# Second branch's keys and queries as four normed pairs with seven quarter products, on one Trainium2 core

## The chip, the core and the metric

The kernel runs on one core of a Trainium2 chip. A core has a matrix engine (TensorE, PE in the profile, with its weight loads PEld), three engines for elementwise work (VectorE or DVE, ScalarE or ACT, GpSimd or POOL) and SyncE (SP), which here only issues transfers. Every engine works through its own queue in order. TensorE writes to PSUM, eight banks of 2 KB in each of 128 partitions; the other memory on the core is SBUF. The metric is the device time of one execution in microseconds, lower is better.

## The reference: one layer of a hybrid encoder

A prompt of 1024 new frames and 64 frames of a running stream (1088 tokens, T in the code) go through one layer of width 1024. The part around the change is the input projection and the per-head norm of the second ("chunk-band", cb) branch:

```python
h = rms_norm(x, norm_w) @ w_in                 # 1024 -> 6144 columns
sb_q, sb_k, sb_v, sb_z, cb_q, cb_k, cb_v, cb_z, g_sb, g_cb = split(h)
cb_q = rms_norm(cb_q.reshape(lead + (8, 64)), q_norm_w)   # per head of 64
cb_k = rms_norm(cb_k.reshape(lead + (8, 64)), k_norm_w)
...
s = q @ k.T * 0.125 + rel_bias[clip(q_pos - k_pos)]       # cb branch
y = x + (sigmoid(g_sb) * b_sb + sigmoid(g_cb) * b_cb) @ w_out
```

The keys and values of both branches are outputs too; of the cb branch only the last 512 prompt frames and the 64 stream frames. Products are held to float32 accuracy: an operand is split into a high part and a low part (the rest of the subtraction), and three of the four products of parts are summed on TensorE.

## The kernel before, in words

Each engine's order is the order in which the code issues its instructions; there is no planner. The work around the change has two stages ahead of the attention.

**The natural stage** (the loop around L466, "natural" since tokens are on the partitions). List `NB` names eight blocks of 256 columns of `w_in`: one of sb values, two of cb keys, two of cb queries, one of sb values, two of cb values. A block runs over nine token tiles (the 64 stream frames first). A tile of 128 frames takes 24 matmuls of 256 columns into one PSUM bank (L466), the stream tile 16. Values are copied out by ACT and stored. Keys and queries go through `evac_nat` (copy, square, per-head sum, `rsqrt` on POOL), `norm_nat` (two multiplications on DVE) and, some tiles later, `post_nat` (two transposes on PE at L351, and the split into high and low part), and are stored transposed to DRAM. During the first block the frames are normed and transposed; the cached keys are transposed in blocks 1 to 4 (`cache_pair`). From the sixth block on `make_t` makes, on DVE and ACT, four sums of quarters of the transposed frames (t0 to t3), with their split.

**The pair stage** (L632 on, the loop at L651). `pairs` lists 14 pairs of 128-column groups: keys and queries of the sb branch, the gates and others. A pair is a product of a 2x2 block matrix of weights (256 columns by 1024) with a 2x2 block matrix of frames (1024 by two halves of 544 tokens). It is done in seven quarter products, s = 0 to 6, in place of eight, at the price of sums: `presum` makes the weight sums on DVE, six products ahead; `prep` splits them on ACT and POOL, five ahead. A quarter product is 2 column chunks (c = 0, 1; 256 and 288 tokens) of 12 matmuls (L672). There are six PSUM banks, three for each chunk, one buffer each: bank 1 takes products 0 and 3, bank 2 takes 1, 4 and 5, bank 3 takes 2 and 6. DVE reads a bank between the products that share it, so the product that comes next into that bank waits on PE until DVE has read. The tightest such place is bank 2 between s = 4 and s = 5: `u3` of chunk 0 (L680) is to be read while PE does chunk 1 of s = 4. Finished results go to `emit`: split, store by SP one product later, and for keys a transposition back through PSUM tile `acc` (pool `psF`, two buffers). From the fifth pair on `dv_step` also makes differences of the sb values.

The relative-position bias is laid out in DRAM as eight arrays of 128 equal rows (`d_rb`), which the attention reads with a skew: `load_rb` spreads the table over 128 partitions, `make_rb` writes the negated and clamped row with DVE and stores it, head by head.

The lines below are the functions that the change touches.

Of the kernel before, what the change touches and what calls it, by code (L numbers as in the profile page):

```python
# [8 lines left out]
F32 = mybir.dt.float32  # L9
# [9 lines left out]
NP = 1024  # L19
# [13 lines left out]
def hybrid_step_kernel(ctx: ExitStack, tc: tile.TileContext, x_prompt, x_sample, c_sbk, c_sbv, c_cbk, c_cbv,  # L33
# [49 lines left out]
    d_o = {b: [dram.tile([128, T], F32, name=f"d_o{b}{p}") for p in range(NPAIR)] for b in ("sb", "cb")}  # L83
    d_rb = [dram.tile([128, 768], F32, name=f"d_rb{h}") for h in range(8)]
# [62 lines left out]
    for p in (0, 2):  # L147
        pairs += [("k", 512 + 128 * p, p), ("q", 128 * p, p)]
# [51 lines left out]
    with ExitStack() as ph:  # L200
        sx = ExitStack()
        natx = sx.enter_context(tc.tile_pool(name="natx", bufs=2))
        pn = ph.enter_context(tc.tile_pool(name="pn", bufs=2, side="right"))
        p1x = ExitStack()
# [5 lines left out]
        NB = [1024, 2560, 2816, 2048, 2304, 1280, 3072, 3328]  # L210
        nb = len(NB)
        xts, xns, hl, cks = {}, {}, {}, {}
# [21 lines left out]
        wqk = pn.tile([128, 2, 64], F32, name="wqk", bufs=1)  # L234
# [3 lines left out]
        def load_rb():  # L238
            rbs[0] = p1.tile([128, 8, 257], F32, name="ck", bufs=1)
            SP.dma_start(rbs[0], rel_bias[0:1].to_broadcast([128, 8, 257]))  # L240

        def make_rb(h):
            rb = rbs[0]
            rx = p1.tile([128, 768], F32, name="rx", bufs=3)
            V.tensor_scalar(rx[:, 0:512], rb[:, h, 256:257].to_broadcast([128, 512]), -1.0, None, op0=OP.mult)
            V.tensor_scalar(rx[:, 512:768], rb[:, h, 255::-1], -1.0, None, op0=OP.mult)
            SP.dma_start(d_rb[h], rx)
# [50 lines left out]
        def evac_nat(i, t, ps):  # L298
            r = rows(t)
            if t == 8:  # L300
                ps = fold(pn, ps)
            c0 = NB[i]
            grp = c0 // 512
            n0 = c0 % 512
            if grp in (2, 6):
                v = pn.tile([128, 256], F32, name="vst", bufs=3)
                A.activation(v[:r], ps[:r, :], AF.Copy)
                dst = d_sbv if grp == 2 else d_cbv
                SP.dma_start(dst[t * 128:t * 128 + r, n0:n0 + 256], v[:r])
                if grp == 2:  # L310
                    SP.dma_start(tok(o_sbv_p, o_sbv_s, t)[:, n0:n0 + 256], v[:r])
                elif t == 8:
                    SP.dma_start(o_cbv_s[:, n0:n0 + 256], v[:r])
                elif t >= 4:
                    SP.dma_start(o_cbv_p[(t - 4) * 128:(t - 3) * 128, n0:n0 + 256], v[:r])
                return
            sq = p1.tile([128, 256], F32, name="sqn")
            ms = p1.tile([128, 4], F32, name="msn")
            rs = p1.tile([128, 4], F32, name="rsn", bufs=3)
            qn = p1.tile([128, 4, 64], F32, name="qn", bufs=5)  # L320
            A.activation(qn[:r].rearrange("p h d -> p (h d)"), ps[:r, :], AF.Copy)
            A.activation(sq[:r], ps[:r, :], AF.Square)
            V.tensor_reduce(ms[:r], sq[:r].rearrange("p (h d) -> p h d", d=64), axis=AX.X, op=OP.add)
            rsqrt(rs[:r], ms[:r], 1.0 / 64, 4)
            return qn, rs

        def norm_nat(i, t, qn, rs):
            r = rows(t)
            n0 = NB[i] % 512
            isk = 1 if NB[i] // 512 == 5 else 0  # L330
            V.tensor_tensor(out=qn[:r], in0=qn[:r], in1=rs[:r, :, None].to_broadcast([r, 4, 64]), op=OP.mult)
            V.tensor_tensor(out=qn[:r], in0=qn[:r], in1=wqk[:r, None, isk, :].to_broadcast([r, 4, 64]),
                            op=OP.mult)
            if isk:
                if t == 8:
                    SP.dma_start(o_cbk_s[:, n0:n0 + 256], qn[:r].rearrange("p h d -> p (h d)"))
                elif t >= 4:
                    SP.dma_start(o_cbk_p[(t - 4) * 128:(t - 3) * 128, n0:n0 + 256],
                                 qn[:r].rearrange("p h d -> p (h d)"))

        def post_nat(i, t, qn):
            r = rows(t)
            c0 = NB[i]
            isk = 1 if c0 // 512 == 5 else 0
            p0 = (c0 % 512) // 128
            if t in (8, 4):
                hl[0] = p1.tile([128, 2, 2, 576], F32R, name="hl", bufs=3)
            h = hl[0]
            pt = psK.tile([128, 2, 128], F32, name="pk")
            for j in range(2):  # L350
                TE.transpose(pt[:, j, :r], qn[:r].rearrange("p h d -> p (h d)")[:, j * 128:(j + 1) * 128],  # L351
                             ident[:r, :r])
            c = 512 if t == 8 else (t % 4) * 128
            o = slice(c, c + r)
            A.activation(h[:, :, 0, o], pt[:, :, :r], AF.Copy)
            V.tensor_tensor(out=h[:, :, 1, o], in0=pt[:, :, :r], in1=h[:, :, 0, o].bitcast(F32), op=OP.subtract)
            dst = (d_kT if isk else d_qT)["cb"]
            if t in (3, 7):
                for j in range(2):
                    rdma(dst[p0 + j][:, :, (t - 3) * 128:(t + 1) * 128], h[:, j, :, 0:512])  # L360
                    if t == 3:
                        rdma(dst[p0 + j][:, :, NP:T], h[:, j, :, 512:576])
# [1211 lines left out]
```

## Time and profile before

| | us |
|---|---|
| median of 3 runs (985.72 to 988.01) | 986.68 |
| the profiled execution | 985.0 |
| its span in the profile | 983.2 |
| granted TensorE clock | 1.0 |

The profile is of one execution. "Busy" is the time in which an engine had an instruction at work; a row of a group of instructions gives the line, the engine, output and inputs by the program's names, partitions by elements, the count, the busy sum and the mean of one in ns, and behind the second bar the idle time ahead of them and what ended it. The chain of work that ended last is followed back from the last instruction. The natural stage runs from the start to 226 us, the pair stage from 226 to 524 us, and the attention and the last products take the rest.

### The profile page before, as it was taken

The numbers are of one execution on the slowest core, as the hardware profiler recorded it, in microseconds if no ns is written. First come the engines' busy times: TensorE is split into PE (matmuls) and PEld (weight loads), VectorE is DVE, ScalarE is ACT, GpSimd is POOL, SyncE is SP. The second block draws the span as 40 slices with busy tenths as digits, with TensorE's granted clock in tenths as the row PEclk, the third lists the DMA queues.
The fourth block names the chain that finished last, engine by engine and source line by source line (L and its number), as shares of the span: only waits on it lengthen the run. The fifth ranks groups of instructions, "written<-read, shape, count | busy, mean of one in ns | idle before, by whom it ended". The sixth has DMA issues, their size and how long they took to land.

```text
span 983.2 us, 20553 instructions
## 1 busy us (share of the span) xinstructions
PE 957.4 (97%) x7620; PEld 913.0 (93%) x7620; DVE 594.5 (60%) x1168; ACT 479.3 (49%) x1056; POOL 394.1 (40%) x389
## 2 busy tenths in 40 slices
PE   5999999999999999999999899998999999999998
PEld 5999999999999999999999788887888887999998
DVE  5456664796454655533322479776677765689745
ACT  6544443344443433433332567666886875466320
POOL 3276664115444576556523100111421101486551
PEclk9999999999999999999999999999999999999999
DMA  6727567533656565565424999667798862762642
GB/s 230 229 89 239 193 234 255 161 98 120 183 178 199 157 184 169 151 196 173 128 73 127 263 225 250 175 185 184 212 269 238 227 177 84 236 201 74 219 131 76
DMA packets 176585, 176.82 MB, mean 180 GB/s; under 512 B 33825, under 2 KB 160669, under 8 KB 176358
## 3 DMA queue, kind: packets, MB, share of 16 engines
q1 hardware_dynamic: 164950, 160.50, 55.7%
q10 hardware_dynamic: 8720, 8.33, 2.6%
q0 software_dynamic: 2816, 6.69, 2.0%
q8 instruction: 60, 0.98, 0.5%
q14 instruction: 39, 0.32, 0.1%
HBM read 113.46 MB, written 62.00 MB: 178 GB/s over the span
## 4 chain that ended last, share of the span: by engine, by line
PE 89%; ACT 3%; DMA 2%; SPq 2%; DVE 2%; issue 1%; POOL 1%; DVEq 0%; ACTq 0%; POOLq 0%
PE b L672 30%; PE acc L466 19%; PE b L1488 8%; PE o L1172 7%; PE pt L1133 6%; PE z L1080 6%; PE b L974 5%; PE acc L932 4%; PE acc L832 2%; SPq L51 1%; ACT wT L1142 1%; DMA wrawx<-in_w_in_dram 1%; PE pk L351 1%; DMA ks<-d_ksbT 1%; PE pt L279 1%
## 5 line engine op out<-in xcount | busy, mean ns | idle before, releaser
L1133 PE MATMUL pt<-ident,be 128*128 128x128 f32 (+1 forms) x568 | 87.5, 278 | 6.2 <-DVE sm L1085 1.8
L1080 PE MATMUL z<-ks,sq 128*128 128x320 f32 (+5 forms) x384 | 84.9, 330 | 1.8 <-DMA sq<-d_qsbT 1.5
L1102 DVE TENSOR_TENSOR_SCAN be<-be,imp 128x128 f32<-128x128 f32 (+7 forms) x64 | 83.4, 1341 | 5.2 <-ACT be L1083 5.1
L1133 PEld LDWEIGHTS pt<-ident,be 128*128 128x128 f32 (+1 forms) x568 | 65.2, 140 | 18.8 <-issue 5.7
L1142 ACT ACTIVATE wT<-pt 128x512 f32<-128x512 f32 (+3 forms) x125 | 57.1, 485 | 49.3 <-PE pt L1133 48.0
L466 PE MATMUL acc<-whi,xa 128*128 128x256 f32 x256 | 74.2, 292 | 0.0
L466 PE MATMUL acc<-wlox,xm 128*128 128x256 f32 x256 | 70.7, 278 | 0.0
L466 PE MATMUL acc<-whi,xm 128*128 128x256 f32 x256 | 70.7, 278 | 0.0
L466 PE MATMUL acc<-wlo,xa 128*128 128x256 f32 x256 | 70.7, 278 | 0.0
L466 PE MATMUL acc<-whix,xb 128*128 128x256 f32 x256 | 70.6, 278 | 0.0
L466 PE MATMUL acc<-whix,xm 128*128 128x256 f32 x256 | 70.6, 278 | 0.0
L680 DVE TENSOR_TENSOR u<-b,s 128x256 f32<-128x256 f32 (+1 forms) x56 | 24.2, 440 | 73.4 <-PE b L672 71.9
L1080 PEld LDWEIGHTS z<-ks,sq 128*128 128x128 f32 x384 | 64.8, 189 | 3.5 <-DMA sq<-d_qsbT 1.2
L1172 PE MATMUL o<-wT,vp 128*64 128x256 f32 (+1 forms) x608 | 66.6, 357 | 0.1
L1172 PEld LDWEIGHTS o<-wT,vp 128*64 128x64 f32 x608 | 43.9, 136 | 22.9 <-issue 5.5
L123 POOL TENSOR_TENSOR wlo<-wraw,whi 128x1024 fp32r<-128x1024 f32 x15 | 36.6, 2437 | 51.6 <-ACT whi L116 46.4
L745 POOL DMA_DIRECT2D d_osb<-zt x20 | 10.8, 542 | 114.3 <-DVE zt L1181 102.9
L1105 ACT ACTIVATE be<-be,sm 128x640 f32<-128x640 f32 (+5 forms) x68 | 47.2, 694 | 9.7 <-DVE sm L1104 9.5
L436 POOL TENSOR_TENSOR whix<-ws,whix 128x512 fp32r<-128x512 f32 x28 | 37.1, 1324 | 32.5 <-ACT whix L435 32.5
L1083 ACT ACTIVATE be<-z 128x384 f32<-128x384 f32 (+6 forms) x104 | 47.2, 492 | 3.9 <-PE z L1080 3.4
L1093 ACT ACTIVATE be<-be,sm 128x640 f32<-128x640 f32 (+5 forms) x68 | 47.2, 695 | 3.5 <-DVE sm L1085 3.0
L466 PEld LDWEIGHTS acc<-whi,xa 128*128 128x128 f32 x256 | 47.9, 188 | 0.1
(306 smaller groups left out, 3196.3 us busy)
## 6 DMA issues: line engine op xcount, KB each, us to landing
wraw<-in_w_in_dram SPq DMA_DIRECT2D x31, 512.0 KB, 4.4
wrawx<-in_w_in_dram SPq DMA_DIRECT2D x17, 512.0 KB, 4.3
sq<-d_qsbT SPq DMA_DIRECT2D x32, 192.0 KB, 6.2
sq<-d_qcbT SPq DMA_DIRECT2D x32, 192.0 KB, 5.4
xt<-in_x_prompt_dram SPq DMA_DIRECT2D x8, 512.0 KB, 5.8
d_kcbT<-hl SPq DMA_DIRECT2D x8, 512.0 KB, 4.4
d_qcbT<-hl SPq DMA_DIRECT2D x8, 512.0 KB, 3.1
d_ksbT<-hl SPq DMA_DIRECT2D x16, 256.0 KB, 2.7
```

The costliest lines, as they stand in the source:

```text
L466: TE.matmul(ps, x, w, start=m == 0, stop=m == len(steps) - 1)
L672: TE.matmul(ps[:, :m], w[:, hl_, k], right[s](x)[:, k, a:b], start=s < 3 and k == 0 and e == 0, stop=k == 3 and e == 2, skip_group_check=s ...
L974: TE.matmul(pp[uu][:, :n], w[:, p, uu * 128:uu * 128 + 128], g[:, a:e], start=p == 0 and m == 0, stop=p == NPAIR - 1 and m == 2)
L1080: TE.matmul(z[:, :m], s[:, e, q0:q0 + 128], ks[:, h, o + x:o + y], start=e == parts[0][0], stop=e == parts[-1][0])
L1083: A.activation(be[:r, x:y], z[:r, :m], AF.Sigmoid, scale=-0.125)
L1093: A.activation(be[:, :n], be[:, :n], AF.Exp, bias=kp[:, j:j + 1], scale=-1.0, accum_out=kp[:, 2:3])
L1102: V.tensor_tensor_scan(be[:r, n - 1::-1], be[:r, n - 1::-1], im[:, ::-1], 0.0, op0=OP.mult, op1=OP.max)
L1105: A.activation(be[:r, :n], be[:r, :n], AF.Copy, scale=kp[:r, 3:4])
L1133: TE.transpose(pt[:kr, x, :r], be[:r, kb * 128:kb * 128 + kr], ident[:r, :r])
L1142: A.activation(w[:, sl:sl + m, q0:q0 + r], pt[:, :m, :r], AF.Copy)
L1172: TE.matmul(o[hd * 64:hd * 64 + 64, c0:c1], vv[:kr, kb, hd * 64:hd * 64 + 64], wT[b, p, j, hd, s // 4][:kr, s % 4, c0:c1] if j < 4 else wT ...
L1488: TE.matmul(ps[:, t], left[s](xs_, k)[:, ts_], wt_[:, k], start=s < 3 and t == k == e == 0, stop=k == 3 and e == 2, skip_group_check=s > 2 ...
```

## The change

The four natural blocks of cb keys and queries go away. In their place stand four more pairs, `ck` and `cq`, in the pair stage, ahead of and between the sb ones: ck, q, ck, q, cq, k, cq, k. What was done with tokens on the partitions is now done with tokens along the row, on pieces of 128 by 256 or 288 (`normed`):

- `squares`: ACT squares the piece and copies it to a high part, POOL makes the low part;
- `spread`: PE multiplies a block matrix of ones by both parts, so that each row gets the sum over its head of 64, and ACT takes the square root (`Sqrt`, from PSUM);
- `scale`: DVE takes the reciprocal of the 128 by 256 or 288 piece, and multiplies piece, weight and reciprocal in one instruction;
- `parts`: ACT and DVE split, SP stores, and keys that are an output are transposed back (`k_out`).

The four run as a pipe: `norm_step`, called eight times in a pair, issues `parts` of the piece that entered four steps ago, `scale` of the one of three steps ago, `spread` of the one of two steps ago, and `squares` of a new one. So eight pieces of a pair are finished in the first part of the pair behind it. `make_t` moves forward to the second of the now four natural blocks; the cached keys go to the second and fourth. `dv_step` starts with the tenth of 18 pairs. The bias table is loaded on 8 partitions, made there once, stored as `d_r8`, and spread to the eight `d_rb` by transfers within DRAM, one in each of the first eight pairs. Buffers change with it (`hl` 7 for 4, `s1` and `u2` 4, `ko` 3, others shared).

```diff
     for p in (0, 2):
-        pairs += [("k", 512 + 128 * p, p), ("q", 128 * p, p)]
+        pairs += [("ck", 2560 + 128 * p, p), ("q", 128 * p, p)]
+    for p in (0, 2):
+        pairs += [("cq", 2048 + 128 * p, p), ("k", 512 + 128 * p, p)]
...
-        NB = [1024, 2560, 2816, 2048, 2304, 1280, 3072, 3328]
+        NB = [1024, 1280, 3072, 3328]
...
+        def make_rb():
             rb = rbs[0]
-            rx = p1.tile([128, 768], F32, name="rx", bufs=3)
...
+            rx = p2.tile([8, 768], F32, name="rx", bufs=1)
+            V.tensor_scalar(rx[:, 0:512], rb[:, 256:257].to_broadcast([8, 512]), -1.0, None, op0=OP.mult)
+            V.tensor_scalar(rx[:, 512:768], rb[:, 255::-1], -1.0, None, op0=OP.mult)
+            SP.dma_start(d_r8, rx)
+
+        def spread_rb(h):
+            SP.dma_start(d_rb[h], d_r8[h:h + 1].to_broadcast([128, 768]))
...
+            def squares():
+                sq = hold[:, 288 * nsq[0]:288 * nsq[0] + n]
+                nsq[0] = (nsq[0] + 1) % 3
+                h = up.tile([128, 2, 288], F32R, name="hl", bufs=HB)
+                A.activation(sq, x, AF.Square)
+                A.activation(h[:, 0, :n], sq, AF.Copy)
+                G.tensor_tensor(out=h[:, 1, :n], in0=sq, in1=h[:, 0, :n].bitcast(F32), op=OP.subtract)
+                return h
+
+            def spread(h):
+                pt = psF.tile([128, 512], F32, name="acc")[:, :n]
+                for e in range(2):
+                    TE.matmul(pt, ones, h[:, e, :n], start=e == 0, stop=e == 1)
+                rt = up.tile([128, 288], F32, name="rt", bufs=2)
+                A.activation(rt[:, :n], pt, AF.Sqrt, bias=eps64)
+                return rt[:, :n]
+
+            def scale(rt):
+                V.reciprocal(rt, rt)
+                V.scalar_tensor_tensor(x, x, wn[:, 1:2] if isk else wn[:, 0:1], rt, op0=OP.mult, op1=OP.mult)
+
+            def parts():
+                h = up.tile([128, 2, 288], F32R, name="hl", bufs=HB)
+                A.activation(h[:, 0, :n], x, AF.Copy)
+                V.tensor_tensor(out=h[:, 1, :n], in0=x, in1=h[:, 0, :n].bitcast(F32), op=OP.subtract)
+                soon(0, lambda: stores(rdma, half, c, h[:, :, :n], dst[:]))
+                if isk and (half or c):
+                    soon(1, lambda: k_out(src, p, half, c, c * 256 if half else None, o_cbk_p, o_cbk_s))
...
+        def norm_step(late):
+
+            pipe[1:] = pipe[:4]
+            pipe[0] = [norms.pop(1 if late and len(norms) > 1 else 0), None] if norms else None
+            for at, k in ((4, 3), (3, 2), (2, 1), (0, 0)):
+                f = pipe[at]
+                if f:
+                    f[1] = f[0][k](*(f[1:] if k in (1, 2) else ()))
...
-                if i > 3:
+                if i > 8:
                     dv_step(n % 2)
+                if i < 8 and s == 0:
+                    spread_rb(i)
                 w = blk.pop(n)
                 for c, (a, b) in enumerate(XC):
                     m = b - a
+                    if c and s != 4:
+                        norm_step(s == 5 or s == 6)
...
+                if s in (2, 6):
+                    norm_step(False)
```

How this moves instructions shows in two places, both in the second pair (a `q` pair). First DVE, from the end of the first pair to the sum `u` that PE needs before it may start s = 5. Before, the whole stretch is nine instructions (the last of the first pair, the weight sums `ws`, two sums of s = 1, the split of the two results of s = 3, and the sum):

```order
L581 TENSOR_TENSOR hl<-u_3343,hl 128x288
L403 TENSOR_TENSOR ws<-wraw,ws 128x512
L680 TENSOR_TENSOR u_3641<-b_3628,s_3606 128x256
L680 TENSOR_TENSOR u_3656<-b_3643,s_3621 128x288
L403 TENSOR_TENSOR ws<-wraw,wrawx 128x512
L403 TENSOR_TENSOR ws<-ws,wraw 128x512
L581 TENSOR_TENSOR hl<-b_3593,hl 128x256
L581 TENSOR_TENSOR hl<-b_3608,hl 128x288
L680 TENSOR_TENSOR u_3758<-b_3628,s_3606 128x256
```

In the changed kernel the same stretch has 25 on DVE; its last twelve are these (`hl` of L554 are the split of the q pair, the rest are steps of the normed pieces of the ck pair):

```order
L616 TENSOR_TENSOR hl<-u_1887,hl 128x288
L610 RECIPROCAL rt<-rt 128x288
L611 SCALAR_TENSOR_TENSOR kf<-kf,wn,rt 128x288
L616 TENSOR_TENSOR hl<-kf,hl 128x288
L610 RECIPROCAL rt<-rt 128x256
L611 SCALAR_TENSOR_TENSOR s_1738<-s_1738,wn,rt 128x256
L554 TENSOR_TENSOR hl<-b_1982,hl 128x256
L616 TENSOR_TENSOR hl<-s_1738,hl 128x256
L610 RECIPROCAL rt<-rt 128x288
L611 SCALAR_TENSOR_TENSOR s_1753<-s_1753,wn,rt 128x288
L554 TENSOR_TENSOR hl<-b_2011,hl 128x288
L711 TENSOR_TENSOR u_2225<-b_2032,s_1995 128x256
```

Six reciprocals of full pieces, six scalings and five splits have come in ahead of the sum. Second PE, in the same pair at the step from s = 2 to s = 3. Before, the matmuls of one product follow those of the other:

```order
L672 MATMUL b_3694<-t0h,whix 128x288 x2
L672 MATMUL b_3694<-t0l,whix 128x288
L672 MATMUL b_3694<-t0h,whix 128x288 x2
L672 MATMUL b_3694<-t0l,whix 128x288
L672 MATMUL b_3694<-t0h,whix 128x288
L672 MATMUL b_3593<-xm,wlox 128x256
```

Now a spread of squares (`ones`) and a transposition back stand between them:

```order
L703 MATMUL b_2111<-t0h,whix 128x288 x2
L703 MATMUL b_2111<-t0l,whix 128x288
L703 MATMUL b_2111<-t0h,whix 128x288
L604 MATMUL acc<-hl,ones 128x288 x2
L572 MATMUL acc<-ident,u_1873 128x128 x2
L703 MATMUL b_1982<-xm,wlox 128x256
```

Both inserted groups need a buffer of `acc` and a result of other engines, and PE's queue holds them in order.

More of the change, by code (lines that the diff above doesn't have):

```diff
@@ L325, in evac_nat @@
[L325 to L362, printed above, removed]
+            v = pn.tile([128, 256], F32, name="vst", bufs=3)
@@ L590, in emit, with k_out @@
                 V.tensor_copy(kf[:, :n], src[:, :n])
[L592 to L595 removed]
+            soon(2 if (w, half) == (0, 0) else 3,
+                 lambda: k_out(kf, p, half, c, half * 512 + c * 256, o_sbk_p, o_sbk_s))
+        def k_out(kf, p, half, c, a, o_p, o_s):
+            pt = psF.tile([128, 512], F32, name="acc")
+            cols = slice(p * 128, (p + 1) * 128)
+            if a is not None:
```

172 lines of the change are left out of this document (89 added, 83 removed).

## The prediction

> **What bounds the kernel now.** I read the page's busy line first, then the chain that ended last by line:
>
> ```profile
> PE 957.4 (97%) x7620; PEld 913.0 (93%) x7620; DVE 594.5 (60%) x1168; ACT 479.3 (49%) x1056; POOL 394.1 (40%) x389
> PE b L672 30%; PE acc L466 19%; PE b L1488 8%; PE o L1172 7%; PE pt L1133 6%; PE z L1080 6%; PE b L974 5%; PE acc L932 4%; PE acc L832 2%; SPq L51 1%; ACT wT L1142 1%; DMA wrawx<-in_w_in_dram 1%; PE pk L351 1%; DMA ks<-d_ksbT 1%; PE pt L279 1%
> ```
>
> PE carries the time, half of it in the two stages that change (L466 natural, L672 pairs). The view by windows says how much the others have left there: one natural block with keys or queries, the end of `make_t`, and a stretch with a q and a k pair.
>
> ```profile
> 127.00:154.00 27.00, 27.00 (x234) 26.80 (x233) 19.15 (x45) 11.26 (x31) 17.76 (x20) 1.00 0.66 230
> 203.00:226.00 23.00, 23.00 (x205) 23.00 (x204) 22.47 (x33) 9.72 (x21) 1.29 (x1) 1.00 0.32 99
> 250.00:275.00 25.00, 25.00 (x205) 24.99 (x204) 11.49 (x24) 9.49 (x24) 10.72 (x7) 1.00 0.70 210
> 275.00:300.00 25.00, 25.00 (x202) 24.54 (x201) 13.41 (x28) 11.21 (x30) 11.55 (x8) 1.00 0.52 156
> ```
>
> Columns: length, then busy PE, PEld, DVE, ACT, POOL, the granted clock, the DMA share. PE is full in all four; its clock is 1.00. In the pairs DVE has about 12 of 25 us left: what the change lays there must fit into that, and where it comes in a bunch, into less.
>
> **What PE gains.** The chain in order of time gives the pitch of both stages (start, duration, what):
>
> ```profile
> 21.36 0.87 PE pt L279 x8
> ...
> 72.85 1.89 PE acc L466 x16
> ...
> 84.44 2.82 PE acc L466 x24
> ...
> 154.37 1.90 PE acc L466 x16
> ...
> 300.44 223.60 PE b L672 x1800
> ```
>
> The x16 pieces are stream tiles, with which a block begins. Three of the four blocks that go lie between 72.85 and 154.37: 81.5 us, 27.2 a block, where 8 x 2.83 + 1.9 = 24.5 is matmuls and the rest transpositions. Twenty of these are of cached keys and only move: at 0.87/8 = 0.109 us, 2.2 us. So 79.3 us for three, 105.8 for four.
>
> A pair is 168 matmuls at 223.60/1800 = 0.124 us: 20.9, four make 83.5. The spreads are 4 x 8 x 2 = 64 matmuls of the same widths, 7.9 us. The keys' transpositions back are 12 a ck pair, 24 x 0.109 = 2.6 us. Together 94.0. PE gains 105.8 - 94.0 = **11.8 us**, if it waits for nothing.
>
> **What DVE has to carry.** These rows price its instructions (groups by form; then three lines of the timeline in a k pair):
>
> ```profile
> L680 DVE TENSOR_TENSOR u<-b,s 128x288 f32<-128x288 f32 x28 | 12.8, 456 | 24.0 <-PE b L672 23.7 <-ACT wlo L435 0.3
> L680 DVE TENSOR_TENSOR u<-b,s 128x256 f32<-128x256 f32 x28 | 11.9, 425 | 49.3 <-PE b L672 48.3 <-ACT s L676 0.8
> L268 DVE SCALAR_TENSOR_TENSOR xn<-xt,rs,nw 128x512 f32<-128x512 f32 x16 | 11.3, 748 | 5.7 <-POOL rs L251 5.6
> L1181 DVE SCALAR_TENSOR_TENSOR zt<-o,vl,zt 128x128 f32<-128x128 f32 x32 | 9.6, 342 | 22.2 <-PE o L1172 19.6 <-PE z L1080 2.6
> L403 DVE TENSOR_TENSOR ws<-ws,wraw 128x512 f32<-128x512 f32 x9 | 11.2, 1242 | 0.3
> L403 DVE TENSOR_TENSOR ws<-wraw,ws 128x512 f32<-128x512 f32 x10 | 8.0, 799 | 2.7 <-POOL whix L436 2.7
> L403 DVE TENSOR_TENSOR ws<-wraw,wrawx 128x512 f32<-128x512 f32 x4 | 4.6, 1140 | 0.0
> L581 DVE TENSOR_TENSOR hl<-u,hl 128x288 fp32r<-128x288 f32 x8 | 3.7, 460 | 5.2 <-ACT hl L580 5.2
> L581 DVE TENSOR_TENSOR hl<-u,hl 128x256 fp32r<-128x256 f32 x8 | 3.4, 426 | 15.2 <-ACT hl L580 15.2
> L590 DVE COPY kf<-b 128x288 f32<-128x288 f32 x2 | 0.9, 448 | 0.0
> L1104 DVE RECIPROCAL sm<-sm 128x1 f32<-128x1 f32 x68 | 10.5, 154 | 2.6 <-ACT be L1093 2.6
> L245 DVE TENSOR_SCALAR rx<-ck 128x512 f32<-128x512 f32 x8 | 3.4, 422 | 4.6 <-DMA d_rb<-rx 4.6
> L246 DVE TENSOR_SCALAR rx<-ck 128x256 f32<-128x256 f32 x8 | 2.3, 285 | 0.0
> L539 DVE TENSOR_SCALAR wqk<-wqk 128x64 f32<-128x64 f32 x1 | 0.2, 177 | 0.0
> ```
>
> ```profile
> 252.58 0.43 DVE L581 TENSOR_TENSOR hl<-u,hl 128x256 fp32r<-128x256 f32 x1 [4.11 <-ACT hl L580]
> 252.92 0.45 DVE L687 TENSOR_TENSOR u<-b,u 128x288 f32<-128x288 f32 x1
> ...
> 266.40 0.43 DVE L581 TENSOR_TENSOR hl<-u,hl 128x256 fp32r<-128x256 f32 x1 [0.53 <-ACT hl L580]
> ```
>
> The large unknown is the *reciprocal* of a 128 by 256 or 288 piece; the trace has it for one element only, 154 ns. With one pass per element, as the step from 425 to 456 ns over 32 elements (1.0 ns each) has it, 288 elements would take 0.44 us. For the other end I take away the fixed part of the nearest instructions with one tensor in SBUF. L245 and L246 give 0.535 ns an element and a fixed 148 ns, which leaves 6 ns for the one element; L539 gives 177 - 64 x 0.535 = 143, which leaves 11. So 1 to 11 ns. I take 6, from the row pair that is measured eight times each: 1.68 us for 256 elements, 1.88 for 288. It is a thin difference of rows, and the forecast hangs on it.
>
> [...]
>
> A scaling lies between the rows of 342 and 748: 0.48 and 0.51 us. Neighbours in the queue that do not depend on each other overlap by 0.09 (252.58 + 0.43 against 252.92).
>
> Now the stretch shown in the order. Let T be the end of the ck pair on PE. From its last sum DVE does, up to `u` of s = 4: six reciprocals 10.7, six scalings 3.0, five splits 2.2, three weight sums 0.80 + 1.14 + 1.24 = 3.2, two splits of the q pair 0.9, two sums of s = 1 0.9, `u` 0.4: 21.3 us. Sixteen overlaps take 1.4 off; two splits that wait for ACT's copy, as at 266.40, add 1.0; the last sum of the ck pair takes 0.4 after T. So `u` is read at T + 21.3. PE does in that time five products (14.9), six spreads (1.5) and six transpositions (0.65) and wants to start s = 5 at T + 17.1. It waits **4.2 us**. Part of that may fall earlier, at a spread whose square stands on ACT behind a copy that waits for a scaling; the end is the same, since DVE sets it.
>
> The transpositions of the last ck piece (`k_out`) stand on PE ahead of s = 1 of the pair after that. Up to their scaling DVE has from `u`: sums and splits of s = 4 to 6 and one weight sum 6.5, two reciprocals 3.6, two scalings 1.0, five waits for ACT 2.7, less 0.9 of overlaps: 12.9, against three products, a spread and a few transpositions on PE, 9.5. Another **3.4 us**.
>
> Behind a cq pair there is no `k_out`: PE has 0.65 less to do up to s = 5, and the k pair adds two copies of 0.41 and 0.45 (L590) ahead of `u`: 4.2 + 0.65 + 0.7 = **5.5 us**. Sum: 2 x (4.2 + 3.4) + 2 x 5.5 = **26.2 us**.
>
> **The rest, at nothing.** ACT in the stretch: five weight copies at 0.63 (row below), and some 25 square roots, squares, copies and splits at 0.44 (L580), 14 of 21 us; the table that `Sqrt` needs is one load more, 1.28. POOL: seven weight parts and eight low parts of squares; it gives up the `rsqrt` of the natural blocks. From the rows below (the square's part like L625) 7 x 1.42 + 8 x 0.83 = 16.6 of 21 us or more:
>
> ```profile
> L435 ACT ACTIVATE wlo<-ws 128x512 fp32r<-128x512 f32 x28 | 17.6, 630 | 40.7 <-DVE ws L403 36.1 <-PE b L672 4.4
> L580 ACT ACTIVATE hl<-u 128x288 fp32r<-128x288 f32 x8 | 3.6, 445 | 8.0 <-DVE u L692 3.6 <-DVE u L687 2.7 <-DMA d_ksbT<-hl 1.7
> L574 ACT ACT_TABLE_LOAD x1 | 1.3, 1283 | 0.0
> L376 DVE TENSOR_TENSOR hc<-pc,hc 128x512 fp32r<-128x512 f32 x8 | 5.4, 679 | 0.0
> L436 POOL TENSOR_TENSOR wlo<-ws,wlo 128x512 fp32r<-128x512 f32 x28 | 39.8, 1420 | 16.4 <-ACT wlo L435 8.9 <-PE acc L466 4.9 <-DMA d_dv<-dva 2.1
> L625 POOL TENSOR_TENSOR dva<-dva,dvb 128x256 f32<-128x256 f32 x24 | 19.9, 830 | 4.5 <-DMA dvb<-d_sbv 4.5
> ```
>
> `make_t` filled DVE to 22.47 of 23 us without PE waiting; now four cached keys fall into it (L376), 3 us, and it has a block more to end in: 0 to 3 us, taken as 0. On SP's queue the stores of a normed piece wait for its split, so weight loads behind them are late by DVE's lag; they are asked for four products (12 us) ahead. The bias rows: sixteen DVE instructions become two small ones, beside full PE both times; the eight writes of 393 KB now are reads as well, one per pair, beside a DMA share of 0.5 to 0.7. `dv_step` still ends some nine products before the stage does.
>
> **The sum.** 985.0 (profiled execution) - 11.8 + 26.2 = 999.4. The median of the runs lies 1.7 above that execution: **1001**.
>
> **Rivals.** *The reciprocal streams* (1 ns an element). Six take 2.6 us in place of 10.7, DVE arrives at T + 13, ahead of PE's 17.1, and nothing waits but a spread now and then, 0 to 3 us in all: 986.7 - 11.8 + 1 = 976. For it: the fixed parts scatter as much as the remainder (L680 gives 177 ns, more than all of the 154). Against: 148 and 143 come from the nearer form. A stretch has 1632 elements under reciprocals, so each ns less takes 1.63 us from each of the four waits, and 0.54 from the later ones, 7.6 in all: at about 4.1 ns the change is worth nothing, below it is a gain.
>
> *The reciprocal is dearer still*, between 6 and the 11 of L539: at 8.5, 2.5 x 7.6 = 19 more, 1020; at 11, 1039. [...]
>
> *DVE's lag is taken up.* If copies and sums run wide apart and the waits overlap with those at spreads, or the price is near 4, the two terms cancel: 985 to 989. Against: the bank between s = 4 and s = 5 has one buffer and 1.5 us of room.
>
> *PE's gain does not come*, because spreads and transpositions wait for `acc`, which has two buffers. Each wait would have to be new, at 64 of them 0.2 us eat the gain; in the wide-open pairs before, PE shows none. It would be 988 to 995 with a cheap reciprocal.
>
> **Chances.** Iterative at about 6: 0.60 (990 to 1012). Dearer: 0.12. Streams: 0.13. Taken up: 0.08. Spreads eat the gain: 0.07. From these, faster by over 0.2% (about what runs of this kernel can tell from no change) 0.18, within it 0.05, slower 0.77. The range leaves out the lowest part of streaming and the highest prices: 978 to 1022; the likeliest case alone gives 990 to 1012.
>
> **What would show it.** L610 reciprocals near 1.7 and 1.9 us; DVE over 9 tenths from about 120 us on for eight pairs; waits of PE at L703 for the sum of L711 or for Sqrt or square parts, 4 to 6 us behind each normed pair; natural stage shorter by 105 us; pair stage longer by about 120. If L610 shows under 1 us, the forecast is wrong by its first step; if it shows 6 ns and PE still runs through, the walk of the stretch is wrong.

## The result, and the profile after

The kernel after takes 1041.99 us (median, 1038.70 to 1045.79), 1.056 times the kernel before (95% interval 1.053 to 1.059): 55 us slower. The profiled execution took 1040.72 us. The forecast had the sign, but 1042 lies outside its 978 to 1022.

The busy line of the page, the chain by line and the row of the granted clock, of the kernel after:

```profile
PE 968.2 (93%) x7476; PEld 919.4 (88%) x7476; DVE 650.4 (63%) x1167; ACT 508.2 (49%) x1118; POOL 382.9 (37%) x373
PEclk9999999998998899999999999999999999999999
PE b L703 19%; PE b L1521 7%; PE o L1205 7%; PE pt L1166 6%; PE z L1113 6%; PE b L1007 5%; PE acc L965 3%; PE acc L865 2%; SPq L51 1%; ACT wT L1175 1%; DMA sq<-d_qsbT 1%; DMA ks<-d_ksbT 1%; DMA gt<-d_gsb 1%; DVE wT L1177 1%; PE acc L1557 1%
```

PE is no longer full, and the share of the pairs (L703) in the chain has fallen from 30 to 19%, though they take longer. The clock is below 9 tenths in three of 40 slices. Before the change its row was:

```profile
PEclk9999999999999999999999999999999999999999
```

The view by windows shows the stretch, in which the new pairs are (columns as in the prediction):

```profile
120.00:175.00 55.00, 48.94 (x392) 48.02 (x391) 39.91 (x55) 26.73 (x62) 29.54 (x25) 1.00 0.42 133
175.00:225.00 50.00, 39.51 (x292) 38.27 (x291) 34.04 (x48) 23.52 (x59) 23.21 (x21) 0.90 0.44 128
225.00:275.00 50.00, 43.94 (x332) 43.24 (x330) 32.12 (x53) 20.90 (x52) 21.31 (x19) 0.93 0.48 145
275.00:325.00 50.00, 37.51 (x249) 36.23 (x250) 30.55 (x50) 18.65 (x50) 17.30 (x14) 0.86 0.45 131
325.00:375.00 50.00, 41.60 (x302) 40.20 (x300) 39.72 (x56) 22.14 (x58) 20.99 (x18) 0.93 0.49 147
```

From 175 us on PE is busy for 37 to 44 of 50 us, and its granted clock is 0.86 to 0.93 there. DVE is not full either: it has 10 to 20 us left in each 50.

The natural stage ends at 122.05 us instead of 226.46 (the first pair's first matmul), 104.4 earlier. The starts of the pairs on PE give their lengths: 21.3 for the first ck, then 30.0, 29.4, 30.0, 30.3, 32.6, 33.1, 32.6 and 29.5, and from the tenth on 20.9 as before. The eight long ones are together 80 us longer than eight plain ones, and outside them hardly anything was lost: the loss of 55 us lies in them. What PE waited for in them is in the view of waits, from 120 to 400 us (instruction, what it waited for, sum, count, longest):

```profile
PE acc L572 <- ACT ko L580: 12.1, 4, 5.6
PE acc L572 <- ACT kos L576: 11.5, 2, 5.8
PE b L703 <- DVE u L711: 7.8, 2, 3.9
PE acc L604 <- ACT rt L606: 5.3, 2, 2.7
PE acc L572 <- ACT rt L606: 3.6, 2, 1.8
PE acc L604 <- ACT hl L597: 2.3, 2, 1.2
PE acc L574 <- ACT rt L606: 1.9, 2, 1.6
PE acc L604 <- POOL hl L598: 1.3, 2, 0.7
```

Together 45.8 us. Only 7.8 of them are the wait that the prediction put first, for the sum `u` at the bank; 29.1 stand at the transpositions of `k_out` (L572, L574), and 8.9 at the spreads (L604).

DVE's groups by form, of the kernel after:

```profile
L610 DVE RECIPROCAL rt<-rt 128x288 f32<-128x288 f32 x16 | 31.1, 1944 | 0.0
L610 DVE RECIPROCAL rt<-rt 128x256 f32<-128x256 f32 x16 | 27.9, 1742 | 0.0
L611 DVE SCALAR_TENSOR_TENSOR u<-u,wn,rt 128x288 f32<-128x288 f32 x8 | 7.5, 934 | 0.3
L611 DVE SCALAR_TENSOR_TENSOR s<-s,wn,rt 128x256 f32<-128x256 f32 x4 | 5.4, 1362 | 0.1
L611 DVE SCALAR_TENSOR_TENSOR u<-u,wn,rt 128x256 f32<-128x256 f32 x8 | 3.9, 485 | 0.3
```

The reciprocal costs (1944 - 1742)/32 = 6.3 ns an element; all 32 take 59.0 us of DVE. A scaling of the same size takes 0.49 us in one place and 1.36 in another; the prediction had 0.48 and 0.51 for all.

### The profile page after: what moved, and what is told of

It reads as the page before. It is cut to its first block, busy times and chain, and to the rows that moved or that the text cites. A ratio compares the mean times of both kernels' runs of the same rounds, so it can differ in the third digit from the quotient of the medians.

```text
span 1038.9 us, 20470 instructions
## 1 busy us (share of the span) xinstructions
PE 968.2 (93%) x7476; PEld 919.4 (88%) x7476; DVE 650.4 (63%) x1167; ACT 508.2 (49%) x1118; POOL 382.9 (37%) x373
## 4 chain that ended last, share of the span: by engine, by line
PE 55%; ACT 3%; DMA 2%; SPq 2%; DVE 1%; issue 1%; POOL 0%; ACTq 0%; POOLq 0%; DVEq 0%
PE b L703 19%; PE b L1521 7%; PE o L1205 7%; PE pt L1166 6%; PE z L1113 6%; PE b L1007 5%; PE acc L965 3%; PE acc L865 2%; SPq L51 1%; ACT wT L1175 1%; DMA sq<-d_qsbT 1%; DMA ks<-d_ksbT 1%; DMA gt<-d_gsb 1%; DVE wT L1177 1%; PE acc L1557 1%
## 5 line engine op out<-in xcount | busy, mean ns | idle before, releaser
L711 DVE TENSOR_TENSOR u<-b,s 128x256 f32<-128x256 f32 x72 | 31.3, 439 | 93.0 <-PE b L703 79.6
L703 PE MATMUL b<-t3h,whi 128*128 128x288 f32 (+1 forms) x288 | 60.4, 296 | 7.8 <-DVE u L711 7.8
L1205 PEld LDWEIGHTS o<-wT,vp 128*64 128x64 f32 x608 | 44.6, 139 | 23.1 <-issue 6.7
L703 PE MATMUL b<-xm,wlox 128*128 128x288 f32 (+1 forms) x288 | 63.5, 307 | 0.0
L405 POOL TENSOR_TENSOR wlo<-ws,wlo 128x512 fp32r<-128x512 f32 x36 | 47.3, 1313 | 37.2 <-ACT wlo L404 37.2
L703 PE MATMUL b<-t1h,wlo 128*128 128x288 f32 (+1 forms) x288 | 60.8, 298 | 0.0
L610 DVE RECIPROCAL rt<-rt 128x256 f32<-128x256 f32 (+1 forms) x32 | 59.0, 1843 | 0.0
L703 PE MATMUL b<-t2h,whix 128*128 128x288 f32 (+1 forms) x288 | 58.0, 290 | 0.0
L703 PE MATMUL b<-xa,whi 128*128 128x288 f32 (+1 forms) x288 | 57.6, 288 | 0.0
L703 PE MATMUL b<-t0h,whix 128*128 128x288 f32 (+1 forms) x288 | 57.6, 287 | 0.0
L703 PE MATMUL b<-xm,wlo 128*128 128x288 f32 (+1 forms) x288 | 56.8, 285 | 0.0
L703 PEld LDWEIGHTS b<-t3h,whi 128*128 128x128 f32 x288 | 48.5, 196 | 8.6 <-DVE u L711 8.6
```

Source lines behind the costliest of these rows:

```text
L405: G.tensor_tensor(out=t[:, 1], in0=src, in1=t[:, 0].bitcast(F32), op=OP.subtract)
L610: V.reciprocal(rt, rt)
L703: TE.matmul(ps[:, :m], w[:, hl_, k], right[s](x)[:, k, a:b], start=s < 3 and k == 0 and e == 0, stop=k == 3 and e == 2, skip_group_check=s ...
L711: V.tensor_tensor(out=u[:, :m], in0=ps[:, :m], in1=s1[c][:, :m], op=OP.add)
L1205: TE.matmul(o[hd * 64:hd * 64 + 64, c0:c1], vv[:kr, kb, hd * 64:hd * 64 + 64], wT[b, p, j, hd, s // 4][:kr, s % 4, c0:c1] if j < 4 else wT ...
```

## The experiments

### The reciprocal, and the buffer of `kos`

The first theory, A: DVE's reciprocals hold everything up, as predicted, and the waits at `k_out` are the same lag met earlier. The rival, B: half of the loss is that `kos` went from two buffers to one (ACT waits 19.4 us in eight pieces for its stores to land). Four kernels:

```diff
 kos2, and in rec1_kos2 and rsabs_kos2 too
-                kos = up.tile([32, 128], F32, name="kos", bufs=1)
+                kos = up.tile([32, 128], F32, name="kos", bufs=2)
 rec1, rec1_kos2
-                V.reciprocal(rt, rt)
+                V.reciprocal(rt[:, 0:1], rt[:, 0:1])
 rsabs_kos2
-                A.activation(rt[:, :n], pt, AF.Sqrt, bias=eps64)
+                A.activation(rt[:, :n], pt, AF.Abs_reciprocal_sqrt, bias=eps64)
-                V.reciprocal(rt, rt)
```

> The changed kernel with two buffers for the small copy `kos` in place of one; nothing else. Theory A (the reciprocals alone make DVE late, and every wait of PE follows from that): no change, 1036 to 1046. Theory B (half of the loss comes from the single `kos` buffer: its store stands behind late stores on SP's queue, ACT stops at the next `kos` for up to 8 us, and PE then has no `acc` buffer): the five waits of about 5.7 us ahead of L572 shrink to under 2, and the slow matmuls behind them go: 1008 to 1022; the waits ahead of L703 for `u` (3.9 us, twice) stay.

Measured: 1040.95 us, ratio 1.0545 (1.0514 to 1.0577). Beside whole reciprocals the second `kos` moves nothing; B falls in this form.

> The changed kernel with the reciprocal taken of one column only (the other columns of the cb branch's norms are then wrong; every instruction is still there): 32 instructions fall from 1.84 to about 0.15 us, 54 us of DVE. Theory A: no wait is left, 972 to 982, faster than before the change. Theory B: DVE is in time, so the waits for `u` go, but two `kos` of one pair still follow each other within a few us of a store that takes 3 to 5: 982 to 1000, with waits of 1 to 4 us ahead of L572.

Measured: 1010.56, ratio 1.0239 (1.0201 to 1.0278). It ran twice, 1007.81 and 1013.32, so differences from it are good to some 3 us. The reciprocals are worth 31 us, but A wanted the whole loss and more to go: this is a miss for both theories.

> Both edits together: reciprocal of one column, two `kos` buffers (norms wrong in the other columns). Both theories: 971 to 980, no wait of PE over 1 us in the eight first pairs, granted clock 1.00 there. If it stays above 985, something third holds PE.

Measured: 1004.72, ratio 1.018 (1.0154 to 1.0206).

> The changed kernel with two `kos` buffers, and ACT's function `Abs_reciprocal_sqrt` from PSUM in place of `Sqrt` on ACT and the reciprocal on DVE: the same work on ACT, 59 us less on DVE. Both theories: 971 to 981 and faster than before the change by 0.5 to 1.5%; ACT's instruction takes 0.45 to 0.50 us like `Sqrt`. If ACT's function is dearer or its table is loaded more than once, 985 or more.

Measured: 1001.93, ratio 1.0143 (1.0122 to 1.0164). With the inverse root from ACT DVE has no reciprocal at all, and the kernel is still 15 us slower than before. Something else takes some 25 us. The three largest waits of PE with one-column reciprocals and two `kos` (120 to 400 us):

```profile
PE acc L572 <- ACT ko L580: 8.2, 2, 5.0
PE acc L572 <- ACT kos L576: 5.2, 2, 2.6
PE b L703 <- DVE u L711: 3.6, 2, 1.8
```

Most is at `k_out`. Where the longest ends, ACT's timeline and then SP's of the same run show why (start, duration; in brackets the idle time ahead and what ended it):

```profile
284.96 0.39 ACT L580 ACTIVATE ko<-acc 128x256 f32<-128x256 f32 x1 [7.46 <-DMA out_dram<-ko]
```

```profile
276.79 1.25 SPq L51 DMA_DIRECT2D d_qcbT<-hl  x2
278.09 0.61 SPq L262 DMA_DIRECT2D d_rb<-d_r  x1
278.81 0.53 SPq L358 DMA_DIRECT2D wraw<-in_w_in_dram  x1
279.44 0.45 SPq L581 DMA_DIRECT2D out_dram<-ko  x1
```

A k pair brings eight `k_out`; the last six are copied from 274.37 to 286.51 us, the stall included. Their copies need a `ko` each, of which there are three; the store of a `ko` that was filled at 274.4 is issued by SP only at 279.44, behind eleven stores of `hl` at some 0.6 us each, a spread of the bias and a weight load. That store takes until 284.96, another 5.5 us, to land. So the fourth copy waits for it, ACT stands for 7.46 us with everything behind it, the two `acc` stay full, and PE stands at the next transposition.

### Without `k_out`, and the bias rows alone

```diff
 nokout, rec1_nokout
-            soon(2 if (w, half) == (0, 0) else 3,
-                 lambda: k_out(kf, p, half, c, half * 512 + c * 256, o_sbk_p, o_sbk_s))
...
-                if isk and (half or c):
-                    soon(1, lambda: k_out(src, p, half, c, c * 256 if half else None, o_cbk_p, o_cbk_s))
```

> The kernel after with the reciprocal of one column only and without any of the 30 calls of `k_out` (neither of the two k outputs' rows from transposes is written; their PE transposes, ACT copies and SP stores are gone). If all that is left beside the reciprocal is the way of the k outputs (acc, ko, kos, SP): 1010.6 less about 27 of waiting and slow matmuls and 8 to 10 of the transposes' own time on PE, 973 to 978. If something else also holds PE in the normed pairs: 985 or more.

Measured: 977.80, ratio 0.9908 (0.9885 to 0.9932). (The kernel has 28 calls of `k_out`, not 30: 24 fill a `ko`, and four a `kos` alone.)

> The kernel after, whole reciprocals, without any call of `k_out`. If the full reciprocals delay PE mainly by DVE's results standing late at `k_out` and at the banks: what the reciprocal costs without k_out is small, 980 to 995. If DVE's late `u` holds the bank whatever happens at `k_out` (the prediction's 5.5 us behind cq pairs and 4.2 in q pairs): 990 to 1010. If the two causes add up independently: 1042 less 35, 1005 to 1010.

Measured: 1008.23, ratio 1.0222 (1.0195 to 1.0249). With 1042.0 and 1010.6 this makes a square: the reciprocals cost 31.4 us with `k_out` and 30.4 without, and `k_out` 33.8 us with reciprocals and 32.8 without. About 8 of these are the transpositions' own time (those of sb keys were there before, when the four pairs with keys or queries took 5.1 more in all than four plain ones, without a wait; the prediction's 2.6 for the new ones come to that), the rest is waiting and the slower matmuls behind it (20.8 and 5.4 us with whole reciprocals, by the table further down).

Without `k_out` what is left of PE's waits is the prediction's own list:

```profile
PE b L699 <- DVE u L707: 17.8, 4, 5.4
PE acc L602 <- ACT hl L595: 4.6, 4, 1.2
PE acc L602 <- POOL hl L596: 2.7, 4, 0.7
```

(L699 and L707 are L703 and L711 of the kernel after.) Four waits for `u`, one behind each normed pair: 3.4, 5.0, 3.9 and 5.4 us, where 4.2, 4.2, 5.5 and 5.5 were predicted. With the waits at the spreads just ahead of them, which the prediction counted in, they are 5.3, 6.8, 5.7 and 7.3.

The other part of the change, by itself in the kernel before:

```diff
-            rbs[0] = p1.tile([128, 8, 257], F32, name="ck", bufs=1)
-            SP.dma_start(rbs[0], rel_bias[0:1].to_broadcast([128, 8, 257]))
+            rbs[0] = p1.tile([8, 257], F32, name="ck", bufs=1)
+            SP.dma_start(rbs[0], rel_bias[0])
...
+                if i < 8 and s == 0:
+                    spread_rb(i)
```

> The kernel before with only the bias rows changed: row table made on 8 partitions, written once as 8 rows, and spread to 128 rows by eight copies within DRAM, one at the start of each of the first eight pairs. By the prediction (bias rows cost nothing): 985 to 988. Rival (the spreads stand in SP's queue ahead of the stores and weight loads of the k and q pairs and delay them): 990 or more.

Measured: 986.50, ratio 1.0004 (0.9989 to 1.0018). The bias rows cost nothing there; its pairs have the lengths of the kernel before.

### The small tiles of `k_out` and their stores

```diff
 rec1_ko4, rec1_k44, k44, rsabs_k44_actq
-                ko = up.tile([128, 2, 128], F32, name="ko", bufs=3)
+                ko = up.tile([128, 2, 128], F32, name="ko", bufs=4)
 rec1_ko4: kos = hold[:32, 864:992], one; the others:
-                kos = up.tile([32, 128], F32, name="kos", bufs=1)
+                kos = hold[32 * (nks[0] % 4):32 * (nks[0] % 4) + 32, 864:992]
+                nks[0] += 1
 rec1_actq, rsabs_k44_actq: both stores of k_out
-                SP.dma_start(...)
+                A.dma_start(...)
 rec1_nostore: both stores of k_out
-                SP.dma_start(...)
```

> The kernel after with the reciprocal of one column only (the norms of the second branch come out wrong) and, beside it, the `ko` tiles back at the four of the kernel before (after has three; `kos`, still one, goes to unused columns of `hold` to make room). Compare 1010.6 us with three. Theory C (in the k pairs six transposed outputs come within 10 us, the fourth copy on ACT finds no free `ko` because SP issues the stores some 5 us late, and PE then waits for `acc`; the trace with one-column reciprocals shows ACT idle 7.5 and 5.7 us there and PE waiting 5.0 and 3.3): 1000 to 1004, these two waits gone with the slow matmuls behind them. Theory D (ACT, in order, stands behind DVE results whatever the number of `ko`): 1009 to 1012.

Measured: 1008.79, ratio 1.0232 (1.0200 to 1.0263). A miss for theory C as it was put. The trace shows that the single `kos` took the part of the missing `ko`: ACT waits 18.7 us for its stores, up to 8.1 at a time. Both tiles have to be had at once:

> The kernel after with the reciprocal of one column only (wrong norms), four `ko` tiles and four `kos` (in unused columns of `hold`). Compare 1010.6 us with three and one, 1004.7 with three and two, 1008.8 with four and one, 977.8 without k_out. Theory C (the small tiles of k_out, held until late stores have landed, stop ACT and so PE; with four and one it was the single `kos` that stopped it, 18.7 us of ACT waits for its store): 988 to 999. Theory D (the number of tiles is not what counts; ACT and `acc` are): 1003 to 1009.

Measured: 994.95, ratio 1.0072 (1.0045 to 1.0098): 15.6 less than with three and one.

> The kernel after with the reciprocal of one column only (wrong norms), and the stores of `ko` and `kos` issued by ACT right behind its copies, not by SP; buffers as in after. If the stores are late because SP's queue is full of `hl` stores and of a weight load that waits for its buffer: 988 to 1000. If a store's own time from issue to landing is what holds the tile: 1004 to 1010. If ACT's issuing delays its copies: above 1011.

Measured: 1002.01, ratio 1.0151 (1.0133 to 1.017), between the ranges: 8.6 of these 15.6 us come from the place in SP's queue, with no buffer added.

> The kernel after with the reciprocal of one column only (wrong norms); `k_out` transposes and copies as in after, but nothing stores `ko` and `kos` (the k outputs' rows are left out), so these tiles are free at once. What is left above the 977.8 us without k_out is the transposes' own time on PE (about 8) and ACT's order. Theory C (stores): 984 to 990. Theory D (ACT in order behind DVE): 995 to 1005.

Measured: 992.31, ratio 1.0058 (1.0038 to 1.0079), between the ranges too. With four and four tiles the stores are nearly out of the way (2.6 us left). The other 14.5 us to 977.8 are the transpositions' own time and what stands in this row of PE's waits and the slow matmuls behind it:

```profile
PE acc L572 <- ACT kos L576: 5.1, 2, 2.6
```

> A version meant to be quick: the inverse root in one ACT operation in place of the square root and DVE's reciprocal, four `ko` and four `kos`, and their stores issued by ACT. The reciprocal's 31 us and the greater part of k_out's 25 gone from 1042: 984 to 992. If only the reciprocal's part goes: 1000 or more.

Measured: 994.91, ratio 1.0082 (1.006 to 1.0104): less than hoped for.

> The kernel after, whole reciprocals, with four `ko` and four `kos` tiles. With one-column reciprocals this took 15.6 us off (1010.6 to 995.0). If reciprocal and small tiles are two causes that add up: 1042 less about 16, 1024 to 1029. If DVE's lag hides the late stores (as two `kos` alone, which moved nothing, lets think): 1036 to 1043.

Measured: 1030.65, ratio 1.0435 (1.0418 to 1.0452), between the two. In the whole kernel the small tiles are worth 11 us, not 16: the waits of 5.6 and 3.4 behind the k pairs go, while those of 5.8 at the normed keys stay.

### Half a reciprocal

```diff
 nokout_half: as nokout, and
-                V.reciprocal(rt, rt)
+                V.reciprocal(rt[:, 0:n // 2], rt[:, 0:n // 2])
```

> The kernel after without any k_out, and the reciprocal of the first half of the columns only (wrong norms): 0.8 to 1.0 us each instead of 1.74 and 1.94. Whole gives 1008.2, one column 977.8. The prediction's model (a wait only where DVE's stretch is longer than PE's, so a threshold and then a steep slope): its slope of 7.6 us per ns an element and the 31 us between the two ends put the threshold at 2.2 ns, and half a reciprocal (3.15 ns an element) at 983 to 987. A price without threshold (each us of DVE costs the same): 991 to 995.

Measured: 998.69, ratio 1.0108 (1.0093 to 1.0123). Both are wrong: half the reciprocal costs 20.9 of 30.4 us. The four waits for `u` are 3.70, 3.72, 4.08 and 4.07, hardly less than with whole ones. From the end of the ck pair to the read of `u` DVE takes 23.7 us with whole, 21.2 with half and 17.7 with one-column reciprocals. Six reciprocals of 0.85 us less would have taken off 5.1; 2.5 came off, since the instructions between them grew. Rows of DVE's timeline with half, and of the same two instructions with whole reciprocals:

```profile
146.92 1.51 DVE L614 TENSOR_TENSOR hl<-kf,hl 128x256 fp32r<-128x256 f32 x1
149.34 1.23 DVE L609 SCALAR_TENSOR_TENSOR u<-u,wn,rt 128x256 f32<-128x256 f32 x1
```

```profile
148.21 0.41 DVE L614 TENSOR_TENSOR hl<-kf,hl 128x256 fp32r<-128x256 f32 x1
150.32 0.48 DVE L609 SCALAR_TENSOR_TENSOR u<-u,wn,rt 128x256 f32<-128x256 f32 x1
```

In the kernel after a long scaling lies beside POOL's work; DVE's rows and then POOL's:

```profile
158.36 0.52 DVE L611 SCALAR_TENSOR_TENSOR kf<-kf,wn,rt 128x288 f32<-128x288 f32 x1
161.61 1.34 DVE L611 SCALAR_TENSOR_TENSOR s<-s,wn,rt 128x256 f32<-128x256 f32 x1
```

```profile
161.40 1.27 POOL L405 TENSOR_TENSOR wlo<-ws,wlo 128x512 fp32r<-128x512 f32 x1
```

The scaling that starts at 161.61 ends at 162.95, 0.28 us after POOL's subtraction, which ends at 162.67; the one at 158.36, with POOL idle, takes 0.52. So it is with all eight scalings of that kernel that took 1.33 to 1.38 us: each began while POOL was at a subtraction, lay beside it for 1.01 to 1.09 us, and ended 0.27 to 0.32 us after it. The other 24 took 0.48 to 0.54, four of them (128x256 of `kf`) with POOL at work all the while. Reciprocals beside POOL, 24 of 32, keep the 1.74 and 1.95 of those alone. A reading of this is that a long reciprocal lets POOL's work pass beside it, and that a shorter one leaves more of DVE's other work beside POOL. No run took POOL's work away, so it is not shown by an experiment.

### The place on PE

Four kernels with four `ko`, four `kos`, and stores from SP. None has the inverse root on ACT with all calls in their old place; the nearest are rec1_k44 (994.95) and rsabs_k44_actq (994.91).

```diff
 rsabs_k44_s2: the inverse root on ACT, and
-                    soon(1, lambda: k_out(src, ...
+                    soon(2, lambda: k_out(src, ...
 rsabs_k44_mid, k44_mid: every k_out into a list kq of its own with the old delay, and
+                    if c:
+                        step(kq)
                     if c and s != 4:
                         norm_step(s == 5 or s == 6)
 rsabs_k44_mid_s2: as rsabs_k44_mid, with delay 2 for the normed keys
```

> Meant to be quick: the inverse root in one ACT operation, four `ko` and four `kos`, stores from SP as in after, and the outputs of the normed keys one step later (delay 2 in place of 1), so that ACT's copies for them no longer stand right behind parts that wait for DVE. If the 5 us of PE's waits at k_out in the q and cq pairs were due to that: 986 to 991. If the wait only moves: 993 to 997.

Measured: 989.85, ratio 1.0031 (1.0018 to 1.0043).

> Meant to be quick: as before it, delays as in after, but each pair of k_outs is issued between the two column parts of a step in place of its start, half a step (1.5 us) later on PE. Waits of 2.3 to 2.8 us become about 1: 988 to 993. If the wait only moves: 994 to 997.

Measured: 985.07, ratio 0.9973 (0.9960 to 0.9985): a little quicker than the kernel before, by 0.15 to 0.40%. What PE still waits for (L705 and L713 are L703 and L711; `wlox` is the name that `hold`, and so `kos`, carries):

```profile
PE b L705 <- DVE u L713: 3.6, 3, 1.7
PE acc L572 <- ACT wlox L577: 2.4, 2, 1.2
PE acc L572 <- ACT ko L581: 2.1, 2, 1.1
```

> Both late places for k_out together (the inverse root on ACT, four `ko` and four `kos`, each pair of k_outs between the column parts of a step, and those of the normed keys one step later). With the half step alone 985.1, with the later step alone 989.9. The half step left PE 1.2 us of waits at k_out in each q pair; a step later should end them: 982 to 984.5. If the wait only moves to the spreads, which share the two `acc`, as it did with the later step alone (1.8 us each): 985 to 988.

Measured: 999.92, ratio 1.013 (1.0115 to 1.0145): the wait moved, and grew. A spread now stands behind the late `k_out` in the ring of two `acc`:

```profile
PE acc L605 <- ACT ko L581: 9.7, 2, 4.9
```

> The kernel after with whole square roots and reciprocals, four `ko` and four `kos`, and each pair of k_outs between the column parts of a step. What the reciprocal alone costs in a kernel whose k outputs stand well: 985.1 with the inverse root on ACT. If the reciprocal costs its 30 us (1008.2 less 977.8) here too: 1013 to 1018. If DVE's lag still meets k_out and the two multiply: 1020 to 1030.

Measured: 1030.70, ratio 1.0447 (1.0432 to 1.0462), the same as k44. With whole reciprocals the better place is worth nothing, since the waits go to the next thing that DVE has late:

```profile
PE b L706 <- DVE u L714: 9.7, 3, 5.4
PE acc L572 <- DVE ws L370: 9.3, 2, 4.8
```

With `k_out` in this place the reciprocal thus costs 45.6 us (1030.7 - 985.1), not 30.

## Why the prediction was right and wrong

For each kernel the rows of PE from 121 to 420 us give two sums: the waits that they show, and what matmuls of L703 took above their normal pitch (0.117 us at 256 columns, 0.133 at 288; counted where a row's pitch is over 1.5 times that).

| kernel | us | waits | slow matmuls |
|---|---|---|---|
| after | 1042.0 | 45.8 | 14.5 |
| k44 | 1030.7 | 37.6 | 12.8 |
| rec1 | 1010.6 | 23.1 | 6.9 |
| nokout | 1008.2 | 25.0 | 9.1 |
| nokout_half | 998.7 | 19.3 | 6.1 |
| rsabs_k44_mid | 985.1 | 8.1 | 1.5 |
| rec1_nokout | 977.8 | 6.4 | 0.4 |

**PE's gain of 11.8: right in the natural stage, near in the pairs.** The natural stage is 104.4 shorter (105.8 said). rsabs_k44_mid less its waits and slow matmuls is 975.5, and 986.7 - 11.8 is 974.9. The same subtraction gives 980 to 982 for the kernel after, k44 and rec1, so there 5 to 7 us lie in neither sum.

**The reciprocal at 6 ns an element: right,** 6.3, but in part by luck: it came from a thin difference of two rows, and the other row, L539, would have given 11. The rival at 1 ns an element falls with L610's 1742 and 1944 ns, and its 976 as well: one-column reciprocals give 1010.6. How DVE gets there ("iterative" and "streams" in the chances) no run shows; what the runs show is the 6.3.

**The waits, 26.2: the place right, the sum short by 19.6.** By place, predicted and measured in the kernel after:

| place | predicted | measured |
|---|---|---|
| q pairs, behind ck | 4.2 + 4.2 | 6.1 + 4.8 |
| `k_out` of the normed keys, ahead of s = 1 | 3.4 + 3.4 | 5.8 + 5.7 |
| k pairs, behind cq | 5.5 + 5.5 | 5.7 + 5.7 |
| `k_out` of the k pairs, in the pairs behind them | 0 | 7.1 + 5.0 |

The first three lines measured 33.8 where 26.2 was said, 7.6 more. The walk over DVE's queue came to T + 21.3 and DVE took 23.6: two of the six scalings, beside POOL, took 1.35 and 1.34 us, where all were priced at what they take alone, which is 1.7 of the 2.3 us. The six reciprocals took 11.1 for 10.7, the weight sums 3.1 for 3.2. POOL's part was looked at only for its own load. "Part of that may fall earlier, at a spread" is what happened in the q pairs.

**The step that failed first is "The rest, at nothing".** It followed SP's queue to the weight loads, but not to the stores that give `ko` and `kos` back, of which the change took one each. These 12.1 us are the fourth line; in k44, with four of each, 2.4 of them are left. The rival that spreads and transpositions wait for `acc` got 0.07 because no pair before showed such a wait. It came true, by way of ACT; and it was set up as another case to the reciprocal, while both happened at once.

**The slow matmuls, 14.5 us, are in no term.** Before the change PE waited for nothing in the pair stage (busy for 298.00 of the 298.00 us from 226 to 524, at a clock of 1.00), so its trace could not show them, and the forecast took its six waits of 3.4 to 5.5 us at their own length alone. The last section has this case's rows.

The 41 us by which the forecast missed are thus 19.6 of waits, 14.5 of slow matmuls, and some 7 that these sums don't hold. Part of the 7 may be clock too: 0.90, 0.93, 0.86 and 0.93 in the four windows of 50 us above make, as an estimate, some 19 us of lost clock against the 14.5 counted, though what of it fell into PE's waits cost nothing. The rest is open.

**The slope of 7.6 us per ns, with nothing below a threshold: wrong.** Half a reciprocal should have given 983 to 987 by it, and gave 998.7. Slow matmuls, 6.1 us, are a part of why; that the rest is the longer scalings and splits beside POOL is a reading of the rows above, not shown by a run. The break-even price of 4.1 ns falls with it, and so does the sign to look for of DVE over 9 tenths: it is busy 6 to 8 tenths of the stretch, and late all the same, since it waits for PE (57.5 us from 120 to 400 us) and ACT (31.6) in between.

**At nothing, and rightly so:** the bias rows (tried in the kernel before only) and `make_t`, whose stage ends within 1.4 us of where it was said to.

## What to carry to other kernels

When work is moved from a stage where tiles are plenty into a full pipeline, price the new instruction, but then walk each small ring of buffers to the store that gives it back, and past everything that stands ahead of that store in its queue. PE's waits cost more than themselves here: in the kernel after, 14.5 us of slow matmuls came beside 45.8 us of waits, while in rsabs_k44_mid seven waits of 0.6 to 1.7 us left the granted clock at 1.00 (from 121 to 420 us). Between these two, several waits of 1 us were better than a few of 5. And what a repair is worth depends on what is late next: the better place of `k_out` gained nothing beside whole reciprocals (1030.65 to 1030.70).

## What was not expected of the hardware

**Behind some of its waits PE ran at a lower clock.** PE's rows in the kernel after, behind a wait of 5.77 us:

```profile
182.61 0.69 PE L572 MATMUL acc<-ident,u 128*128 128x128 f32 x2 [5.77 <-ACT kos L576]
...
183.16 0.56 PE L703 MATMUL b<-t1h,wlo 128*128 128x256 f32 x1
183.52 0.41 PE L703 MATMUL b<-t1l,wlo 128*128 128x256 f32 x1
183.74 0.63 PE L703 MATMUL b<-t1h,wlo 128*128 128x256 f32 x2
...
187.54 0.28 PE L703 MATMUL b<-t0l,whix 128*128 128x256 f32 x1
187.66 0.40 PE L703 MATMUL b<-t0h,whix 128*128 128x256 f32 x2
```

From 183.52 to 183.74 is 0.22 us for one matmul; four microseconds later it is 0.12. The product behind the wait takes 4.27 us in place of 3.0. The length of a wait does not settle it in these runs. At 1.79 us it went both ways in one execution, with one-column reciprocals and two `kos`; the two rows of two matmuls stand some 2 us behind their waits:

```profile
261.49 0.38 PE L703 MATMUL b<-t3h,whi 128*128 128x256 f32 x1 [1.79 <-DVE u L711]
...
263.51 0.43 PE L703 MATMUL b<-t3h,whi 128*128 128x288 f32 x2
...
317.67 0.39 PE L703 MATMUL b<-t3h,whi 128*128 128x256 f32 x1 [1.79 <-DVE u L711]
...
320.23 0.68 PE L703 MATMUL b<-t3h,whi 128*128 128x288 f32 x2
```

The granted clock is 1.00 from 260 to 267 us and 0.76 from 316 to 323. Two waits of 2.59 us (to 174.05 and to 223.06) differ in the same way. And with one-column reciprocals and one `kos` a wait of 3.53 us left the pitch alone:

```profile
174.72 0.44 PE L572 MATMUL acc<-ident,u 128*128 128x128 f32 x2 [3.53 <-ACT kos L576]
...
175.34 0.40 PE L703 MATMUL b<-t1h,wlo 128*128 128x256 f32 x2
```

So the matmuls were slower once behind a wait of 1.79 us, and once not behind one of 3.53 us. What else decides, no run shows.

**Some of DVE's scalings took 0.8 to 0.9 us more beside POOL's subtractions,** eight of 32 in the kernel after: 1.33 to 1.38 us against 0.48 to 0.54 for the others, with the rows above. The 24 reciprocals beside POOL took what the other eight did, 1.74 and 1.95. Why, no run shows.
